# Bias rows of the neighbourhood attention loaded as 219 numbers in a row, and other rooms for the values and keys of the context's second quad

## The chip, the core and the metric

The kernel runs on one core of one Trainium2 chip. The core has TensorE (PE in the profile; PEld is its weight load), VectorE (DVE), ScalarE (ACT), GpSimd (POOL) and SyncE (SP), which here only issues DMAs. Each engine works through its own list of instructions in order and waits on semaphores; 16 DMA engines serve the transfers that SP, ACT and POOL issue. The metric is device time in microseconds (us) of one execution; lower is better.

## The reference, cut to what matters

A two-layer backbone works on 256 latent tokens (a grid of 4 rows x 64 columns) and 256 context tokens, 2048 features, fp32. The first layer joins two mixers; the change lies in both.

```python
# gated DeltaNet, 8 heads of 128, two directions; first over the context from a zero state,
# then over the latent tokens from the context's final state
def step(s, xc):                       # per chunk of 64 tokens
    v_new = u_c - einsum('bhik,bhkv->bhiv', w_c, s)
    s_next = s * exp(gl_c) + einsum('bhik,bhiv->bhkv', kd_c, v_new)   # keys and values of the chunk
# neighbourhood attention, 8 heads: every query sees all 4 grid rows, 16 columns, and all context keys
bias = rpb[:, dr[:, None, :, None], dc[None, :, None, :]]      # rpb: (8, 15, 31)
s_loc = einsum(q, k_window) * scale + bias
s_loc = where(in_win, s_loc, -inf)
p = softmax(concatenate([s_loc, q @ k_ctx]))
o = p_loc @ v_window + p_ctx @ v_ctx
```

Then come the output projection, a SwiGLU block, a short convolution layer and a second SwiGLU block, all large matmuls with weights read from HBM.

## The kernel before

**The matmul streams.** Weights come in tiles of 512 KB (`raw`, 4 buffers, loaded by SP at L235). ACT rounds each to `whi` (L175) and DVE forms the remainder `wlo` (L249), 3 buffers each; three products (high x high, high x low, low x high) give fp32 accuracy. The names KB, VB, QB and ZA are the streams of the attention's keys, values, queries and the DeltaNet's output gate; each takes eight tiles (ZA sixteen). The QB streams use 24 half-width matmuls (L347) for each tile. VB runs twice (L302, L303, L307, its last groups L319), and its results are staged in `nst` (3 buffers, copied at L170 or L172) and stored to `vb_d` (L1260). `araw`/`acc` (L435, L441, L443) is a side job: DVE sums the modulation weights while the streams run.

**The DeltaNet work between the streams.** A plan (`P_INV`) starts pieces of it after given steps of the streams. Heads go in two quads of four (q = 0, 1). `chunk_matrices(0)` prepares the latent chunks: DVE solves small triangular systems step by step (L1036 and L1038, tiles `sub_tmp` and `dgs`), which read `lsol`, loaded by SP in eight DMAs (L1027) from a DRAM tile `dl`; the solution goes back to DRAM in `dz` (L1045). `inverses` joins blocks (PE L1092, L1099, L1105; DVE L1107; ACT L1109) for one quad. `scan(q, 1, ...)` runs the context's recurrence of quad q: `kT`, `ktok` and `vtok` are loaded (L961, L956), then four steps of PE L1150 (value products), ACT L1154, PE L1158 (the state's update from `ktok`), DVE L1163, and from the third step on PE L1130 and DVE L1133 (tile `R`, from `vtok`). Both quads follow one another, and the latent quads later. `ktok` and `vtok` have one room each, so the second quad's loads wait until the first quad's last readers are done.

**The neighbourhood attention.** For each head `bias_rows` loads 6 x 64 numbers into each of 128 partitions, in two DMAs of 64 partitions (L1310), from the bias table: partition p starts p numbers further on, and the six pieces lie 31 numbers apart. `na_scores` adds the column mask in place on DVE (L1320), and PE adds the sum to the scores (L1324, L1325). The first head's bias load is issued once the VB stream has given up the memory in which the attention's tiles lie.

**What sets the order.** The tile framework schedules the instructions of all engines at build time, by simulated due times: a change of one room or one transfer changes the order on every engine. At run time each engine's order is fixed, and the SP list is one queue: a DMA that waits for a semaphore holds all those behind it.

Of the kernel before, what the change touches and what calls it, by code (L numbers as in the profile page):

```python
# [23 lines left out]
F32 = mybir.dt.float32  # L24
F32R = mybir.dt.float32r
AF = mybir.ActivationFunctionType
OP = mybir.AluOpType
# [84 lines left out]
def body(tc, x, c, ctx, c_ctx, ada_w, ada_b, norm_mix, norm_ffn, ffn_w_gate, ffn_w_up, ffn_w_down,  # L112
# [3 lines left out]
    PE, ACT, DVE, POOL, SP = nc.tensor, nc.scalar, nc.vector, nc.gpsimd, nc.sync  # L116
# [23 lines left out]
    def pool(name, bufs=1, stack=root, **kw):  # L140
        if kw.get("space") is not bass.MemoryType.DRAM:
            kw.setdefault("reuse_waits", "tile")
        p = stack.enter_context(tc.tile_pool(name=name, bufs=bufs, **kw))
        return p if "space" in kw else Rows(p)
# [15 lines left out]
    def smt():  # L160
        small.append(small.pop(0))
        return small[0].tile([128, 512], F32, name="sm", tag="sm")
# [11 lines left out]
    def acopy(dst, src):  # L174
        ACT.activation(dst, src, AF.Copy)  # L175
# [8 lines left out]
    def C(n):  # L184
        o, w = CO[n]
        return cs[:, o:o + w]
# [356 lines left out]
    def gdt():  # L543
        return gdp.tile([128, 512], F32, name="gd", tag="gd")
# [18 lines left out]
    p = smt()  # L563
# [114 lines left out]
    kd = dram.tile([128, 4, 8, 128], F32, name="kd")  # L678
    vd_ = dram.tile([128, 4, 8, 128], F32, name="vd_")
# [4 lines left out]
    def hslice(d_, t0, n, q):  # L684
        return d_[:, t0:t0 + n, q * 4:q * 4 + 4, :].rearrange("p t h e -> p t (h e)")
# [125 lines left out]
    for b in range(8):  # L811
# [4 lines left out]
        p = smt()  # L816
# [119 lines left out]
    def g4(name, tag, bufs=1):  # L936
        return gw.tile([128, 1024], F32, name=name, tag=tag, bufs=bufs)

    def g2(name, bufs=G2):
        return gw.tile([128, 4, 128], F32, name=name, tag="m2", bufs=bufs)  # L940
# [10 lines left out]
        ACT.activation(em, pD.rearrange("p (i e) -> p i e", i=4), AF.Exp)  # L951
        return em

    def load_tok(tag, d_, t0, q):
        t = g4(tag, tag).rearrange("p (t h e) -> p t h e", t=2, h=4)
        SP.dma_start(t.rearrange("p t h e -> p t (h e)"), hslice(d_, t0, 2, q))  # L956
        return t

    def load_feat(tag, src, pool_=None, bufs=1):
        t = (pool_ or gw).tile([128, 1024], F32, name=tag, tag=tag, bufs=bufs).rearrange("p (h t) -> p h t", h=4)  # L960
        SP.dma_start(t, src)  # L961
        return t
# [149 lines left out]
    def scan(q, seq, xdT, AT=None, qT=None, kT=None, o_t=None):  # L1112

        hs = [q * 4 + i for i in range(4)]
        if kT is None:
            kT = load_feat("kT", kTd[:, seq, q * 4:q * 4 + 4, :])
        ktok = load_tok("ktok", kd, 2 * seq, q)
        vtok = load_tok("vtok", vd_, 2 * seq, q)
        visited = set()
        for step in range(2):  # L1120
            for d in range(2):
                ti = step if d == 0 else 1 - step
                tt = 2 * seq + ti
                tok = slice(ti * 128, ti * 128 + 128)
                zero = seq and step == 0
                sv = state[:, d, q * 4:q * 4 + 4, :]
                if not zero:
                    pP = gdt()
                    for i in range(4):
                        PE.matmul(pP[:, i * 128:(i + 1) * 128], kT[:, i, tok], sv[:, i, :], start=True, stop=True)  # L1130
                    R = g2("R")
                    for i in range(4):
                        DVE.scalar_tensor_tensor(R[:, i, :], pP[:, i * 128:(i + 1) * 128],  # L1133
                                                 negegc[:, d, tt, hs[i]:hs[i] + 1], vtok[:, ti, i, :],
                                                 op0=OP.mult, op1=OP.add)
                if not seq:
                    pQ = gdt()
                    for i in range(4):
                        PE.matmul(pQ[:, i * 128:(i + 1) * 128], qT[:, i, tok], sv[:, i, :], start=True, stop=True)
                    for i in range(4):  # L1140
                        o = o_t[:, ti, i, :]
                        e = eg[:, 0, d, tt, hs[i]:hs[i] + 1]
                        if tt in visited:
                            DVE.scalar_tensor_tensor(o, pQ[:, i * 128:(i + 1) * 128], e, o, op0=OP.mult, op1=OP.add)
                        else:
                            ACT.activation(o, pQ[:, i * 128:(i + 1) * 128], AF.Copy, scale=e)
                pY = gdt()
                for i in range(4):
                    rhs = vtok[:, ti, i, :] if zero else R[:, i, :]
                    PE.matmul(pY[:, i * 128:(i + 1) * 128], xdT[:, d * 8 + ti * 4 + i, :], rhs, start=True, stop=True)  # L1150
                if seq or step == 0:
                    vd = g2("vd")
                    for i in range(4):
                        ACT.activation(vd[:, i, :], pY[:, i * 128:(i + 1) * 128], AF.Copy,  # L1154
                                       scale=brest[:, d, tt, hs[i]:hs[i] + 1])
                    pS = gdt()
                    for i in range(4):
                        PE.matmul(pS[:, i * 128:(i + 1) * 128], ktok[:, ti, i, :], vd[:, i, :], start=True, stop=True)  # L1158
                    if zero:
                        acopy(sv, pS.rearrange("p (i e) -> p i e", i=4))  # L1160
                    else:
                        for i in range(4):
                            DVE.scalar_tensor_tensor(sv[:, i, :], sv[:, i, :], eg[:, 2, d, tt, hs[i]:hs[i] + 1],  # L1163
                                                     pS[:, i * 128:(i + 1) * 128], op0=OP.mult, op1=OP.add)
                if not seq:
                    vn = g2("vn")
                    for i in range(4):
                        ACT.activation(vn[:, i, :], pY[:, i * 128:(i + 1) * 128], AF.Copy,
                                       scale=beta[:, d, tt, hs[i]:hs[i] + 1])
                    pA = gdt()  # L1170
                    for i in range(4):
                        PE.matmul(pA[:, i * 128:(i + 1) * 128], AT[:, d * 8 + ti * 4 + i, :], vn[:, i, :], start=True, stop=True)
                    ov = o_t[:, ti]
                    DVE.tensor_tensor(ov, ov, pA.rearrange("p (i e) -> p i e", i=4), op=OP.add)
                visited.add(tt)
# [12 lines left out]
    lgo = pool("gdn_out", stack=lgs, side="right")  # L1188
# [110 lines left out]
    nap = pool("na", stack=nastk)  # L1299
    yhi[1] = gw.tile([128, 4, 256], F32R, name="yhi1", tag="ktok", bufs=1)  # L1300
    ylo[1] = pool("y_lat", stack=lgs, side="right").tile([128, 4, 256], F32R, name="ylo1")
    bandf = C("band")
    bqs, scaled = {}, []

    def bias_rows(h):
        bq = bqs[h] = nap.tile([128, 6, 64], F32, name="bq", tag="bq", bufs=3)
        for half in range(2):
            src = bass.AP(tensor=ev_rpb.tensor, offset=ev_rpb.offset + h * 465 + (5 - half) * 31 + 15 - 63,
                          ap=[[1, 64], [31, 6], [1, 64]])
            SP.dma_start(bq[half * 64:half * 64 + 64], src)  # L1310

    def na_scores(h):
        kb = nap.tile([128, 512], F32, name="kb", tag="kb", bufs=2)
        qb = pairs[h // 2][:, h % 2, :]
        SP.dma_start(kb, kb_d[:, h, :])
        bq = bqs.pop(h)
        if h < 7:
            bias_rows(h + 1)
        with tc.issue_after(scaled[-1]) if scaled else Stack():
            DVE.tensor_tensor(bq, bq, bandf[:, None, :].to_broadcast([128, 6, 64]), op=OP.add)  # L1320
        out_ = []
        for t in range(2):
            p = smt()
            PE.matmul(p, qb[:, t * 128:(t + 1) * 128], kb, start=True, stop=False)  # L1324
            PE.matmul(p[:, 0:256], C("flip"), bq[:, 2 - 2 * t:6 - 2 * t, :].rearrange("p s c -> p (s c)"),  # L1325
                      start=False, stop=True)
            s = nap.tile([128, 512], F32, name="s", tag="s", bufs=4)
            m = nap.tile([128, 1], F32, name="m", tag="m", bufs=4)
            DVE.tensor_reduce(m, p, axis=AX.X, op=OP.max, negate=True)
            l = nap.tile([128, 1], F32, name="l", tag="l", bufs=4)  # L1330
            ACT.activation(s, p, AF.Exp, bias=m, accum_out=l)
            DVE.reciprocal(l, l)
            scaled.append(DVE.tensor_scalar(s, s, l, None, op0=OP.mult).ins)
            out_.append(s)
        return out_
# [29 lines left out]

    urgent[0] = True
    bias_rows(0)
    queries(0)
    held = na_scores(0)
    for h in range(8):  # L1370
        if h == 3:
# [266 lines left out]
    for half in range(2):  # L1638
# [8 lines left out]
        for f in range(8):  # L1647
            k = half * 8 + f
            p = smt()
# [64 lines left out]
```

## Time and profile before

| | us |
|---|---|
| median of 3 runs (lowest to highest) | 2704.55 (2703.65 to 2706.68) |
| profiled execution, its own time | 2704.46 |
| span of the profile, first to last instruction | 2702.7 |
| TensorE busy | 2643.9 (98% of the span) |
| VectorE busy | 1914.9 (71%) |
| ScalarE busy | 1275.3 (47%) |
| DMA, mean over the span | 253 GB/s |
| mean granted TensorE clock | 0.995 |

The profile is one execution. A group's line gives the source line (L...), the engine, the operation, its output and inputs, the count, the busy time and the mean of one; behind the bar or in brackets stands the engine's idle time before it and what ended it. The list of waits gives, for each pair, the total, the number of times and the longest. The granted clock is the share of TensorE's full clock that its throttle allowed.

### The profile page before, as it was taken

The numbers are of one execution on the slowest core, as the hardware profiler recorded it, in microseconds if no ns is written. First come the engines' busy times: TensorE is split into PE (matmuls) and PEld (weight loads), VectorE is DVE, ScalarE is ACT, GpSimd is POOL, SyncE is SP. The second block draws the span as 40 slices with busy tenths as digits, with TensorE's granted clock in tenths as the row PEclk, the third lists the DMA queues.
The fourth block names the chain that finished last, engine by engine and source line by source line (L and its number), as shares of the span: only waits on it lengthen the run. The fifth ranks groups of instructions, "written<-read, shape, count | busy, mean of one in ns | idle before, by whom it ended". The sixth has DMA issues, their size and how long they took to land.

```text
span 2702.7 us, 37494 instructions
## 1 busy us (share of the span) xinstructions
PE 2643.9 (98%) x13775; PEld 2181.4 (81%) x13775; DVE 1914.9 (71%) x2645; ACT 1275.3 (47%) x1848; POOL 47.1 (2%) x73
## 2 busy tenths in 40 slices
PE   6999999989999999999999999999999999999998
PEld 4688888888888888888888878888788888888886
DVE  4378798856698866776788878898575655545665
ACT  3258633334455444444455563444454444445554
POOL 0000101100000000000000000000000000000000
PEclk9999999999999999999999999999999999999999
DMA  9955688986596978888887859997577777666553
GB/s 368 356 157 177 186 274 263 302 266 186 184 336 230 340 280 289 296 288 287 281 293 260 301 173 337 334 339 253 170 251 224 235 228 238 211 200 213 195 194 110
DMA packets 285148, 682.71 MB, mean 253 GB/s; under 512 B 56957, under 2 KB 98581, under 8 KB 283555
## 3 DMA queue, kind: packets, MB, share of 16 engines
q1 hardware_dynamic: 278636, 667.14, 73.8%
q10 hardware_dynamic: 4423, 9.50, 1.0%
q0 software_dynamic: 1904, 3.67, 0.4%
q8 instruction: 108, 1.77, 0.3%
q14 instruction: 77, 0.63, 0.1%
HBM read 658.16 MB, written 22.05 MB: 252 GB/s over the span
## 4 chain that ended last, share of the span: by engine, by line
PE 92%; DMA 3%; DVE 2%; ACT 1%; issue 1%; SPq 0%; DVEq 0%; ACTq 0%
PE mm L302 21%; PE mm L307 21%; PE mm L303 21%; PE mm L347 11%; PE mm L319 8%; PE sm L194 2%; DMA araw<-in_ada_w_dram 1%; PE sm L605 1%; DVE wlo L249 1%; PE gd L347 1%; PE gd L949 1%; PE sm L1324 1%; PE gd L1150 1%; PE sm L1348 0%; DMA xn<-in_ctx_dram 0%
## 5 line engine op out<-in xcount | busy, mean ns | idle before, releaser
L249 DVE TENSOR_TENSOR wlo<-raw,whi 128x1024 fp32r<-128x1024 f32 x800 | 972.5, 1223 | 456.3 <-ACT whi L175 444.9
L175 ACT ACTIVATE whi<-raw 128x1024 fp32r<-128x1024 f32 x800 | 843.9, 1062 | 856.5 <-PE mm L307 632.9
L302 PE MATMUL mm<-whi,fhi 128*128 128x512 f32 x1232 | 481.9, 393 | 2.6 <-DVE fhi L1471 2.6
L303 PE MATMUL mm<-wlo,fhi 128*128 128x512 f32 x1232 | 479.7, 390 | 0.5 <-DVE wlo L249 0.5
L307 PE MATMUL mm<-whi,flo 128*128 128x512 f32 x1232 | 390.0, 390 | 0.0
L407 DVE SCALAR_TENSOR_TENSOR acc<-araw,cT,acc 128x1024 f32<-128x1024 f32 x224 | 286.8, 1281 | 35.7 <-DMA araw<-in_ada_w_dram 30.7
L302 PEld LDWEIGHTS mm<-whi,fhi 128*128 128x128 f32 x1232 | 231.3, 188 | 50.8 <-DVE fhi L1471 3.9
L307 PEld LDWEIGHTS mm<-whi,flo 128*128 128x128 f32 x1232 | 231.1, 188 | 48.4
L303 PEld LDWEIGHTS mm<-wlo,fhi 128*128 128x128 f32 x1232 | 231.3, 188 | 47.8 <-DVE wlo L249 1.2
L302 PE MATMUL mm<-whi,ahi 128*128 128x512 f32 x664 | 259.0, 390 | 0.0
L303 PE MATMUL mm<-wlo,ahi 128*128 128x512 f32 x664 | 258.3, 389 | 0.0
L347 PE MATMUL mm<-hB,whi 128*128 128x512 f32 (+1 forms) x840 | 234.5, 366 | 1.0 <-DVE hB L629 1.0
L307 PE MATMUL mm<-whi,alo 128*128 128x512 f32 x664 | 206.5, 389 | 0.0
L347 PEld LDWEIGHTS mm<-hB,whi 128*128 128x128 f32 x840 | 147.8, 189 | 24.5 <-DVE hB L629 2.3
L178 ACT ACTIVATE ahi<-prodT 128x256 fp32r<-128x256 f32 x176 | 73.0, 418 | 182.9 <-PE mm L303 179.3
L347 PE MATMUL mm<-hB,wlo 128*128 128x512 f32 (+1 forms) x420 | 149.8, 365 | 0.0
L307 PEld LDWEIGHTS mm<-whi,alo 128*128 128x128 f32 x664 | 124.7, 188 | 25.9
L302 PEld LDWEIGHTS mm<-whi,ahi 128*128 128x128 f32 x664 | 124.7, 188 | 25.8
L303 PEld LDWEIGHTS mm<-wlo,ahi 128*128 128x128 f32 x664 | 124.7, 188 | 25.6
L441 DVE SCALAR_TENSOR_TENSOR acc<-araw,cT,acc 128x512 f32<-128x512 f32 x180 | 133.9, 747 | 4.2 <-DMA araw<-in_ada_w_dram 3.4
L302 PE MATMUL mm<-whi,dhi 128*128 128x512 f32 x336 | 131.1, 393 | 1.2 <-DVE dhi L1471 1.2
L303 PE MATMUL mm<-wlo,dhi 128*128 128x512 f32 x336 | 130.7, 390 | 0.0
(410 smaller groups left out, 3516.4 us busy)
## 6 DMA issues: line engine op xcount, KB each, us to landing
araw<-in_ada_w_dram SPq DMA_DIRECT2D x288, 512.0 KB, 5.2
raw<-in_ffn_w_down_dram SPq DMA_DIRECT2D x176, 512.0 KB, 4.6
raw<-in_ffn_w_gate_dram SPq DMA_DIRECT2D x160, 512.0 KB, 4.4
raw<-in_ffn_w_up_dram SPq DMA_DIRECT2D x160, 512.0 KB, 4.5
raw<-in_ev_w_in_dram SPq DMA_DIRECT2D x112, 512.0 KB, 4.9
araw<-in_ada_w_dram SPq DMA_DIRECT2D x192, 256.0 KB, 4.9
raw<-in_od_w_in_dram SPq DMA_DIRECT2D x96, 512.0 KB, 5.1
raw<-in_ev_w_out_dram SPq DMA_DIRECT2D x32, 512.0 KB, 6.4
```

Of the source, the lines that this page charges most:

```text
L175: ACT.activation(dst, src, AF.Copy)
L178: ACT.activation(hi, src, AF.Copy)
L194: return PE.transpose(dst, src, ident[:n, :n])
L249: last_lo[0] = DVE.tensor_tensor(lo, raw, hi, op=OP.subtract).ins
L302: PE.matmul(ps[ti][n], a, hi[:, n * 512:(n + 1) * 512], start=first, stop=False)
L303: ins = PE.matmul(ps[ti][n], a, lo[:, n * 512:(n + 1) * 512], start=False, stop=False).ins
L307: last_mm[0] = PE.matmul(ps[ti][n], b, hi[:, n * 512:(n + 1) * 512], start=False, stop=False).ins
L319: ins = PE.matmul(ps[ti][n], a(t), w[:, c_], start=False, stop=a is ll and hi is group[-1][0]).ins
L347: last_mm[0] = PE.matmul(o, wt, h_(slice(0, len(ws)), mv, k), start=i == 0 and g == 0 and j == 0, stop=i == len(ks) - 1 and g == len(group ...
L407: DVE.scalar_tensor_tensor(acc, raw, cT[:, k:k + 1], acc, op0=OP.mult, op1=OP.add)
L441: DVE.scalar_tensor_tensor(accs[n], raws.pop(i), cT[:, k:k + 1], accs[n], op0=OP.mult, op1=OP.add)
L605: ins = PE.matmul(pr[32 * j:32 * j + 32, :], cT2[:, g + j, :], raw[:, j].rearrange("p s n -> p (s n)"), start=g == 0, stop=g == KT - 4).ins
```

## The change

`bias_rows` now loads 219 numbers in a row into each partition (tile `br`, 224 wide, 3 rooms): the six pieces of 64 that lie 31 apart overlap, and together they cover 5 x 31 + 64 = 219 numbers. The mask is added from overlapping windows of `br` into a tile `bq` of its own (2 rooms). In `scan`, the context's second quad gets other rooms: its keys go into the room `lsol` (free once the triangular solution is stored), its values into a room of `o_t` (two rooms; the preparation of the latent chunks used it for `n64`, and the latent outputs use it later).

```diff
-    def load_tok(tag, d_, t0, q):
-        t = g4(tag, tag).rearrange("p (t h e) -> p t h e", t=2, h=4)
+    def load_tok(tag, d_, t0, q, room=None):
+        t = (g4(tag, tag) if room is None else room).rearrange("p (t h e) -> p t h e", t=2, h=4)
...
-        ktok = load_tok("ktok", kd, 2 * seq, q)
-        vtok = load_tok("vtok", vd_, 2 * seq, q)
+        ktok = load_tok("lsol" if seq and q else "ktok", kd, 2 * seq, q)
+        vtok = load_tok("vtok", vd_, 2 * seq, q, lgo.tile([128, 1024], F32, name="vtok1", tag="o_t", bufs=2) if seq and q else None)
...
     def bias_rows(h):
-        bq = bqs[h] = nap.tile([128, 6, 64], F32, name="bq", tag="bq", bufs=3)
+        br = bands[h] = nap.tile([128, 224], F32, name="br", tag="br", bufs=3)
         for half in range(2):
             src = bass.AP(tensor=ev_rpb.tensor, offset=ev_rpb.offset + h * 465 + (5 - half) * 31 + 15 - 63,
-                          ap=[[1, 64], [31, 6], [1, 64]])
-            SP.dma_start(bq[half * 64:half * 64 + 64], src)
+                          ap=[[1, 64], [1, 219]])
+            SP.dma_start(br[half * 64:half * 64 + 64, 0:219], src)
+
+    def windows(br):
+
+        return bass.AP(tensor=br.tensor, offset=br.offset, ap=[list(br.ap[0]), [31, 6], [1, 64]])
...
-        bq = bqs.pop(h)
+        bq = nap.tile([128, 6, 64], F32, name="bq", tag="bq", bufs=2)
...
-            DVE.tensor_tensor(bq, bq, bandf[:, None, :].to_broadcast([128, 6, 64]), op=OP.add)
+            DVE.tensor_tensor(bq, windows(bands.pop(h)), bandf[:, None, :].to_broadcast([128, 6, 64]), op=OP.add)
```

The order changes on all engines in this part of the program. Three places matter.

On SP, ahead of the load of `lsol` for the triangular solution (the second quad's values are `vtok_4466` in the changed kernel):

```order
 L235 DMA raw<-in_ev_w_in_dram 128x2x512
 L961 DMA qT<-qTd 128x1024
+L956 DMA vtok_4466<-vd__152 128x2x512
 L1027 DMA lsol<-dl 16x32x32 x8
 L235 DMA raw<-in_ev_w_in_dram 128x2x512
```

The second quad's values now stand ahead of the eight loads of `lsol`, long before the scan.

On SP at the end of the VB stream, before:

```order
L1066 DMA xd<-dz 32x16x32 x2
L235 DMA raw<-in_ev_w_in_dram 128x2x512
L1066 DMA xd<-dz 32x16x32 x2
L1260 DMA vb_d<-nst 128x512
L435 DMA araw<-in_ada_w_dram 128x512
L1260 DMA vb_d<-nst 128x512 x2
L961 DMA kT<-kTd 128x1024
L1310 DMA bq<-in_ev_rpb_dram 64x6x64 x2
L956 DMA vtok<-vd__152 128x2x512
```

The same place in the changed kernel:

```order
L956 DMA lsol<-kd 128x2x512
L1066 DMA xd<-dz 32x16x32
L235 DMA raw<-in_ev_w_in_dram 128x2x512
L1066 DMA xd<-dz 32x16x32 x3
L435 DMA araw<-in_ada_w_dram 128x512
L1260 DMA vb_d<-nst 128x512 x3
L1310 DMA br<-in_ev_rpb_dram 64x219 x2
L1319 DMA kb<-kb_d 128x512
L961 DMA kT<-kTd 128x1024
```

The second quad's keys (`lsol<-kd`) have moved up ahead of `xd`, its values are gone from here, and the first head's bias rows stand ahead of `kT`, no longer behind it.

On DVE at the first bias addition, before:

```order
L1163 SCALAR_TENSOR_TENSOR state<-state,eg,gd 128x128 x4
L1133 SCALAR_TENSOR_TENSOR R<-gd,negegc,vtok 128x128 x4
L172 COPY nst<-mm 128x512
L249 TENSOR_TENSOR wlo<-raw,whi 128x1024
L441 SCALAR_TENSOR_TENSOR acc<-araw,cT,acc 128x512 x2
L1320 TENSOR_TENSOR bq<-bq,cs 128x384
L249 TENSOR_TENSOR wlo<-raw,whi 128x1024
```

And in the changed kernel:

```order
L1163 SCALAR_TENSOR_TENSOR state<-state,eg,gd 128x128 x4
L249 TENSOR_TENSOR wlo<-raw,whi 128x1024
L441 SCALAR_TENSOR_TENSOR acc<-araw,cT,acc 128x512
L1133 SCALAR_TENSOR_TENSOR R<-gd,negegc,vtok 128x128 x4
L172 COPY nst<-mm 128x512
L441 SCALAR_TENSOR_TENSOR acc<-araw,cT,acc 128x512
L1324 TENSOR_TENSOR bq<-br,cs 128x384
L249 TENSOR_TENSOR wlo<-raw,whi 128x1024
```

One `wlo` has moved ahead of `R`; in both orders 83 `wlo` stand ahead of the first bias addition, and the 84th directly behind it.

More of the change, by code (lines that the diff above doesn't have):

```diff
@@ L1302, in body @@
     bandf = C("band")
-    bqs, scaled = {}, []
+    bands, scaled = {}, []
     def bias_rows(h):
-        bq = bqs[h] = nap.tile([128, 6, 64], F32, name="bq", tag="bq", bufs=3)
+        br = bands[h] = nap.tile([128, 224], F32, name="br", tag="br", bufs=3)
         for half in range(2):
             src = bass.AP(tensor=ev_rpb.tensor, offset=ev_rpb.offset + h * 465 + (5 - half) * 31 + 15 - 63,
-                          ap=[[1, 64], [31, 6], [1, 64]])
-            SP.dma_start(bq[half * 64:half * 64 + 64], src)
+                          ap=[[1, 64], [1, 219]])
+            SP.dma_start(br[half * 64:half * 64 + 64, 0:219], src)
+    def windows(br):
+        return bass.AP(tensor=br.tensor, offset=br.offset, ap=[list(br.ap[0]), [31, 6], [1, 64]])
     def na_scores(h):
```

## The prediction

> **What bounds the kernel now.** I read the chain that ended last, then TensorE's waits, then the stretch of the longest one. The page first:
>
> ```profile
> span 2702.7 us, 37494 instructions
> PE 92%; DMA 3%; DVE 2%; ACT 1%; issue 1%; SPq 0%; DVEq 0%; ACTq 0%
> ```
>
> TensorE is the bound. The change takes no matmul away, so it can only return time in which TensorE stands still or runs at a reduced clock. TensorE's waits from 480 to 760 us, which hold everything that the change touches:
>
> ```profile
> PE gd L1150 <- DMA vtok<-vd__152: 7.2, 1, 7.2
> PE gd L1099 <- issue: 2.0, 1, 2.0
> PE gd L1105 <- issue: 1.8, 1, 1.8
> PE mm L347 <- DVE nst L172: 0.4, 1, 0.4
> ```
>
> The longest is the second quad's first product in `scan`, which waits for that quad's values. The chain in order of time and the granted clock there (columns: stretch, length, PE busy, clock, DMA share, GB/s):
>
> ```profile
> 552.14 2.87 PE mm L347 x24
> 555.01 0.67 PE gd L1150 x6
> 556.60 12.23 DMA vtok<-vd__152
> 568.87 2.07 PE gd L1150 x8
> 570.94 11.16 PE mm L347 x79
> 583.00 0.89 PE gd L1150 x8
> ...
> 562.00:564.00 2.00, 0.00 (x0) 1.00 0.65 121
> 564.00:566.00 2.00, 0.00 (x0) 0.61 1.03 384
> 572.00:574.00 2.00, 2.00 (x12) 0.50 0.50 64
> 574.00:576.00 2.00, 2.00 (x16) 0.83 0.85 272
> ```
>
> The values are issued at 556.60, when the one room is free, and come 12.23 us later. The idle array loses half its clock, and the half clock lasts some 6 us into the work that follows. Why they come so late shows in SP's list and in what the DMA engines moved from 557.5 to 563 us:
>
> ```profile
> 554.17 0.72 SPq L961 DMA_DIRECT2D kT<-kTd  x1
> 555.07 1.43 SPq L1310 DMA_DIRECT2D bq<-in_ev_rpb_dram  x2
> 556.60 0.56 SPq L956 DMA_DIRECT2D vtok<-vd__152  x1
> ...
> DMA packets 786, 0.50 MB, mean 90 GB/s; under 512 B 703, under 2 KB 703, under 8 KB 786
> ```
>
> Just ahead of the values stand the first head's bias rows: 2 x 64 x 6 = 768 pieces of 256 bytes. For 5.5 us nearly every packet is a small one, and the engines deliver 90 GB/s.
>
> **Part one, other rooms.** The second quad's values move from 556.60 to directly behind `qT` (470.76 below). A 512 KB transfer issued 85 us ahead of its reader is there in any case, so the wait goes: -7.21 us (568.87 less the end of the work before it; the list rounds to 7.2). The half clock behind it goes too: the first eight products cost 2.07 against 0.89 at full clock (-1.18), and the 79 matmuls 11.16 against 79 x 2.87 / 24 = 9.45 (-1.71). Together -10.10 us.
>
> A rule on the clock: the Trainium skill (TensorE: Matmul & The Clock Gate, Part 1: The HAM clock gate) says that the array falls to half clock after an idle window of about 3.4 us and needs about 3.4 us of work to rise. By that the half clock would cost at most 1.7 us instead of 2.89, an estimate from that page, and the whole 8.9. The rows decide: half clock from 568.87 to beyond 574.
>
> The keys go into the room of `lsol`, and SP waits at that load until `lsol` is stored in `dz`. Before, the next row on SP waited for the same store, so I cost it at nothing:
>
> ```profile
> SPq L1066 <- DMA dz<-lsol: 5.2, 1, 5.2
> ...
> 470.76 0.51 SPq L961 DMA_DIRECT2D qT<-qTd  x1
> 471.69 8.45 SPq L1027 DMA_DIRECT2D lsol<-dl  x8
> ...
> DMA packets 3512, 1.16 MB, mean 193 GB/s; under 512 B 3130, under 2 KB 3136, under 8 KB 3512
> ...
> 482.70 0.21 DVE L1036 TENSOR_TENSOR sub_tmp<-lsol,dgs 128x31 f32<-128x31 f32 x1 [1.96 <-DMA lsol<-dl]
> 516.19 1.29 DVE L1107 TENSOR_SCALAR xd<-gd 32x256 f32<-32x256 f32 x3
> 518.93 1.14 PE L1092 MATMUL gd<-xd,n 64*64 64x64 f32 x30
> ```
>
> What the move costs: the values stand ahead of the eight `lsol` loads, for which DVE already waits 1.96 us. 512 KB at the 193 GB/s of 478 to 484 us take 2.7 us; at the 384 of the best stretch above, 1.4. DVE is late by that much in the triangular solution, and all behind it on DVE with it. TensorE feels it first at L1107: that ends at 517.48 and its reader L1092 starts at 518.93, 1.45 us of cover. So 0 to 1.25 us; I take 0.6, the middle, as nothing tells the ends apart. Were the cover gone, all 2.7 would count. The `wlo` lie up to three tiles ahead of TensorE, so there I cost it at nothing.
>
> The other new waits, each behind work done long before: `ylo` of the attention now waits for the last read of the second quad's keys, and the latent output for the last read of its values; both belong to scans that stand earlier on TensorE than their writers. I cost them at nothing.
>
> **Part two, bias rows.** The sixteen loads stay sixteen issues on SP. The addition keeps 384 numbers; out of place instead of in place I take the same 0.55 us, within 0.1 either way, beside a DVE that has idle time (below). The pieces shrink from 768 to 128 for each head, the bytes from 197 KB to 112 KB. What it is worth hangs on DVE:
>
> ```profile
> L1310 SPq DMA_DIRECT2D bq<-in_ev_rpb_dram x16: 601/610/697, 555.1 to 662.4; - x16
> L1320 DVE TENSOR_TENSOR bq<-bq,cs x8: 551/552/559, 565.9 to 707.2; 128x384 f32<-128x384 f32 x8
> 565.91 0.56 DVE L1320 TENSOR_TENSOR bq<-bq,cs 128x384 f32<-128x384 f32 x1 [6.57 <-DMA bq<-in_ev_rpb_dram]
> 566.38 1.22 DVE L249 TENSOR_TENSOR wlo<-raw,whi 128x1024 fp32r<-128x1024 f32 x1
> 557.70 1.06 ACT L175 ACTIVATE whi<-raw 128x1024 fp32r<-128x1024 f32 x1 [0.44 <-PE mm L347]
> ```
>
> DVE stood 6.57 us for the bias, to 565.91, with the 84th `wlo` behind it, although its `whi` was made at 557.70. TensorE did not feel that, since it stood for the values. With these present it runs on and needs the 84th tile (the QB stream's fourth, since 80 go into the streams before) at 552.14 + 3 x 2.87 + 3 x 0.89 (one product and one update of the first quad, one product of the second) + 0.43 for `nst` = 563.9. The addition and the split take 567.60 - 565.91 = 1.69, so the bias must land by 562.2.
>
> When will it? Two things pull it forward. It no longer stands behind `kT`: 512 KB, 1.4 us at 384 GB/s. And its pieces: if time goes with their number, 5.5 x 128 / 768 = 0.9 us, so 565.91 - 1.4 - 4.6 = 559.9; if with the bytes, 5.5 x 112 / 197 = 3.1, so 562.1. Both make it, the second barely. I take 0 us, with 0 to 5.6 in the range (first rival).
>
> Are the engines able to feed a faster stretch? PE, PEld, DVE, ACT, POOL, clock, DMA share, GB/s:
>
> ```profile
> 552.00:582.00 30.00, 22.36 (x164) 21.95 (x163) 14.46 (x23) 8.63 (x14) 1.81 (x1) 0.83 0.85 247
> 582.00:612.00 30.00, 30.00 (x369) 27.58 (x371) 21.80 (x45) 14.88 (x33) 2.76 (x2) 1.00 0.91 274
> ```
>
> DVE is half idle in the first stretch. DMA moves 7.4 MB there; in 20 us that would be 370 GB/s, too much, but 1 MB of it (second quad's keys and values) is moved out ahead, and 320 GB/s with fewer small packets lies under the 384 seen. I cost the weights at nothing.
>
> **Sum.** -7.21 - 1.18 - 1.71 + 0.6 = -9.5 us against the profiled execution's 2704.46 (1.76 outside its span), which lies 0.09 under the median of the runs: 2695.0.
>
> **Rivals.**
>
> *The bias takes the place of the values (0.14).* If the bias lands as late as before, at 565.91, TensorE waits from 563.9 for a `wlo` until 567.6: 3.7 us, and 1.9 for the clock (between the 0.74 that the row below shows and 2.89). That leaves 3.9 of 9.5: 2700.6. For it speaks that 256-byte pieces were slow for another reason than their number: later, other small packets pass far faster, 1153 in 2.5 us (second row). The Trainium skill (DMA: Bandwidth & Descriptors, Why small descriptors are slow) gives a 256-byte packet only 27% overhead; by that rule fewer pieces would save little more than the bytes, which is the 562.1 above, on the edge. No row shows 876-byte pieces.
>
> ```profile
> 612.45 1.82 issue
> DMA packets 1199, 0.24 MB, mean 95 GB/s; under 512 B 1153, under 2 KB 1153, under 8 KB 1199
> 614.59 2.66 PE sm L1348 x8
> 634.65 1.92 PE sm L1348 x8
> ```
>
> *The two stops without a releaser go as well (0.10).* TensorE stops 1.82 and 1.96 us amid runs of tiny matmuls, and the products after the first cost 2.66 instead of 1.92. The first stands in a stretch full of small packets. Without both: 3.8 + 0.7 more, 2690.5. Against it: the new order puts the same tiny matmuls as close together as the old.
>
> *`lsol` comes much later (0.05), and the kernel is slower.* If the values ahead of it take 12.23 us there as in the row above, DVE's solution, its store, SP's wait on that store and the bias behind it all move by 12.23; the bias then lands at 572.1, 9.9 us too late, and with 2.9 for the clock the gain of 10.1 turns into a loss of 2.7: 2707.2. It decides from a delay of 9.5 us on, and exceeds 0.2% from 14.9. Against it: no bias stands ahead of them at 470 us, and 384 GB/s would bring them in 1.4.
>
> **The numbers.** The forecast has 0.71, with 2692.5 to 2698 as its own range. The range runs from 2689.5, the second rival without the 0.6, to 2701, the first. 0.2% is 5.4 us, about what a measurement tells from no change: faster than 2699.1 are the forecast and the second rival, 0.81, less 0.01 for late weights; the first is within it, and half of the third: 0.15; slower 0.05.
>
> **What would show it.** Right: no wait of L1150 for `vtok`, a clock of 1.00 throughout 560 to 580, a bias load that lands in under 6 us, DVE's wait at the first addition under 3 us, under 200 packets below 512 bytes in the QB stream's first 10 us. Wrong: a wait of L347 for `wlo` after the first bias addition, a wait of L1092 for L1107 near 518, or of TensorE for `whi` later in QB, which would mean that weights became the bound.

## The result and the profile after

| | before | whole change |
|---|---|---|
| median on the chip of the prediction (20 runs each) | 2707.52 us | 2697.49 us |
| ratio (95% interval) | | 0.9967 (0.9959 to 0.9975) |
| the same, measured again twice (5 runs beside 23 each time) | 2708.73, 2707.12 us | 0.9964 (0.9952 to 0.9976), 0.9958 (0.9946 to 0.9970) |
| profiled execution: span, its own time | 2702.7, 2704.46 us | 2698.6, 2700.74 us |

The change saves 9 us, and between 7 and 11 (from the ratio; the two medians lie 10.0 apart). The three runs shown ahead of the prediction are among these twenty of the kernel before, whose median lies 3 us higher, so differences count, not absolute times.

The page of the profile after, its span and its chain by engine:

```profile
span 2698.6 us, 37488 instructions
PE 90%; DVE 3%; DMA 3%; ACT 1%; SPq 1%; issue 1%; DVEq 0%; ACTq 0%
```

TensorE is still the bound. Its waits from 480 to 760 us, the list that stood at the head of the prediction:

```profile
PE mm L347 <- DVE nst L172: 3.4, 1, 3.4
PE gd L1130 <- DMA kT<-kTd: 1.0, 1, 1.0
PE mm L347 <- issue: 0.6, 1, 0.6
PE gd L1150 <- DVE R L1133: 0.2, 1, 0.2
```

The 7.2 us for the second quad's values are gone, and of the two stops without a releaser (2.0 and 1.8) 0.6 is left. In their place stands a stop of L347 for `nst`, which was 0.4. The chain in order of time, then SP's list, then DVE's rows show where it comes from (the change moves the line numbers behind L1310 by 4):

```profile
543.57 13.35 DMA dz<-lsol
```

```profile
557.00 0.38 SPq L956 DMA_DIRECT2D lsol<-kd  x1
558.47 2.05 SPq L1066 DMA_DIRECT2D xd<-dz  x3
561.15 3.62 SPq L1260 DMA_DIRECT2D vb_d<-nst  x3
564.86 1.22 SPq L1310 DMA_DIRECT2D br<-in_ev_rpb_dram  x2
```

```profile
566.62 0.69 DVE L172 COPY nst<-mm 128x512 f32<-128x512 f32 x1 [6.10 <-DMA vb_d<-nst]
568.99 0.56 DVE L1324 TENSOR_TENSOR bq<-br,cs 128x384 f32<-128x384 f32 x1 [1.02 <-DMA br<-in_ev_rpb_dram]
```

`dz` takes 13.35 us to be stored. SP stands at the keys' load into `lsol` until then (8.9 us), and behind that row in the same list stand the loads of `xd` and the stores of `nst`. DVE cannot write the next `nst` until a room is free, and TensorE cannot start the next product. SP's rows in the kernel before:

```profile
549.66 0.86 SPq L1066 DMA_DIRECT2D xd<-dz  x2
552.19 0.43 SPq L1260 DMA_DIRECT2D vb_d<-nst  x1
553.19 0.89 SPq L1260 DMA_DIRECT2D vb_d<-nst  x2
```

By the time it reaches this part, the profile after runs 5.13 us later than the profile before (see below). Without that shift its first store of `nst` goes out at 556.0, which is 3.8 us later than before.

A second new wait lies far behind the change, at the end of the output projection:

```profile
844.13 1.26 PE L450 MATMUL sm<-cs,acc 128*128 128x1 f32 x8 [2.45 <-DVE acc L441]
846.57 0.63 PE L319 MATMUL mm<-wlo,yhi 128*128 128x512 f32 x1
```

The side job's last sum comes 2.45 us late, and the products behind run at half clock (0.63 for one in place of 0.39). In the new order this L450 stands 8 rows ahead of the next block's first product on TensorE, in the old one 36.

That the saving arises in the stretch that the change touches shows from the store of `n` (L1021) to the first product with `fhi`, one row of the kernel before and one of the profile after. Columns: stretch, its length, PE busy with its count, PEld, DVE, ACT, POOL, clock, DMA share, GB/s:

```profile
466.11:853.10 386.99, 372.32 (x3008) 318.60 (x3006) 286.46 (x535) 165.01 (x335) 12.75 (x14) 0.98 0.79 256
```

```profile
471.24:849.10 377.86, 369.74 (x3009) 317.58 (x3007) 288.25 (x536) 165.28 (x337) 13.37 (x14) 0.99 0.78 262
```

The same work takes 9.13 us less: TensorE stands 8.12 us instead of 14.67, and is busy 2.58 less. In the two other profiles of the whole change (`both` and `both2` below) it takes 375.3 and 375.4 us. Behind the stretch the two executions shown differ by 0.1 us (1849.6 and 1849.5). The start of the second row lies 5.13 later, and the two others of the whole change begin at 467.55 and 465.65: that shift arises ahead of the stretch and differs from run to run of one kernel, so it is not the change's.

### The profile page after: what moved, and what is told of

Same layout as the page of the kernel before. It is cut to its first block, busy times and chain, and to the rows that moved or that the text cites. A ratio compares the mean times of both kernels' runs of the same rounds, so it can differ in the third digit from the quotient of the medians.

```text
span 2698.6 us, 37488 instructions
## 1 busy us (share of the span) xinstructions
PE 2646.0 (98%) x13775; PEld 2183.0 (81%) x13775; DVE 1915.9 (71%) x2645; ACT 1274.9 (47%) x1848; POOL 47.8 (2%) x73
## 4 chain that ended last, share of the span: by engine, by line
PE 90%; DVE 3%; DMA 3%; ACT 1%; SPq 1%; issue 1%; DVEq 0%; ACTq 0%
PE mm L302 21%; PE mm L307 21%; PE mm L303 21%; PE mm L347 10%; PE mm L319 8%; PE sm L194 2%; PE sm L605 1%; PE gd L347 1%; DMA araw<-in_ada_w_dram 1%; DMA dz<-lsol 1%; DVE acc L441 1%; PE sm L1328 0%; PE gd L949 0%; DMA xn<-in_ctx_dram 0%; DVE wlo L249 0%
## 5 line engine op out<-in xcount | busy, mean ns | idle before, releaser
L347 PE MATMUL mm<-hB,whi 128*128 128x512 f32 (+1 forms) x840 | 234.6, 366 | 1.0 <-DVE hB L629 1.0
L347 PEld LDWEIGHTS mm<-hB,whi 128*128 128x128 f32 x840 | 147.7, 189 | 24.5 <-DVE hB L629 2.3
L347 PE MATMUL mm<-hB,wlo 128*128 128x512 f32 (+1 forms) x420 | 149.7, 365 | 0.0
```

The source lines that it names most:

```text
L347: last_mm[0] = PE.matmul(o, wt, h_(slice(0, len(ws)), mv, k), start=i == 0 and g == 0 and j == 0, stop=i == len(ks) - 1 and g == len(group ...
```

## The experiments

Twelve runs in three groups, two of them of the whole change itself (`both`, `both2`); each group has its own runs of the kernel before. Gains in us are (1 - ratio) x 2708, with the interval's ends behind.

**The parts apart.** One kernel with the rooms alone, one with the bias rows alone, one with the whole change but for the keys' room:

```diff
 rooms:        only load_tok, and the two loads in scan
 bias:         only bias_rows, windows, na_scores
 values_bias:  the whole change, with
-        ktok = load_tok("lsol" if seq and q else "ktok", kd, 2 * seq, q)
+        ktok = load_tok("ktok", kd, 2 * seq, q)
```

> The whole change again, as the yardstick for the other kernels on this chip. Both theories: 0.9967 of the kernel before, within 0.0008; TensorE without a wait of L1150 for vtok, but with a stop of about 3.4 us of L347 for nst L172 near 563 us (SP's list stands 9 us at the load of lsol for the store of dz, and the stores of nst stand behind it), and a clock near 0.92 after it.

> Rooms alone, bias rows as 6 x 64 pieces as before. SP's order is that of the whole change but for two bias loads. Theory A (the prediction's step 'part two is worth nothing'): as fast as the whole change within 1 us, 0.9967; the bias lands later, but TensorE stands for nst anyway and does not feel it. Rival B (the prediction's first rival): the first bias load takes 8 us instead of 4, DVE stands at the first addition until about 573 us instead of 569, a wlo behind it is late, L347 waits 2 to 4 us for wlo and the clock falls: 3 to 5 us slower than the whole change, 0.998 to 0.9985.

> Bias rows alone, rooms as before. SP's order is that of the kernel before. The second quad's values still wait for their room and are issued at about 556.6 behind the bias. Theory A: with 128 pieces instead of 768 ahead of them they land sooner by what the small pieces took less what 128 pieces take, 2.4 us (by bytes) to 4.6 us (by count): TensorE's wait for vtok is 2.6 to 4.8 us instead of 7.2 and the half clock mostly stays: 2.4 to 6 us gained, 0.9978 to 0.9991. Rival C (the bias has nothing to do with the values being late, the busy DMA engines alone hold them): within 0.5 us of before, 0.9998 to 1.

> The whole change without the keys' room: the second quad's keys stay in the room ktok, so their load stands some 20 places later on SP, behind the bias rows and the loads of xdT. Theory A (the prediction priced the keys' move at nothing because the next row on SP waits for the same store): the stop for nst stays at 3.4 us within 0.5, no other stop appears, time as the whole change within 1 us. Rival D (the keys' room is worth its place): the load comes at about 577 us and lands 4 to 6 us later, L1158 of the second quad waits for ktok 4 to 6 us, 4 to 7 us slower than the whole change. Rival E (the load of lsol is itself what holds the stores of nst): the stop for nst is under 2 us and the kernel 2 to 4 us faster than the whole change.

| | ratio | gain, us |
|---|---|---|
| whole change | 0.9964 (0.9952 to 0.9976) | 9.7 (6 to 13) |
| rooms | 0.9987 (0.9978 to 0.9996) | 3.5 (1 to 6) |
| bias | 0.9981 (0.9970 to 0.9991) | 5.1 (2 to 8) |
| values_bias | 0.9963 (0.9951 to 0.9975) | 10.0 (7 to 13) |

The whole change's stop for `nst` was 0.4 us in this profile, where 3.4 had been expected, and 1.5 us of waiting for `R` came behind it; in the third profile it was 3.4 again. The stop is real and varies from run to run.

*Rooms alone* has the same order on SP in this stretch, but for two bias loads. TensorE's waits from 560 to 640, then the landing of its sixteen bias loads (least, median, most) and that of the whole change:

```profile
PE gd L1150 <- ACT state L175: 4.3, 1, 4.3
PE mm L347 <- DVE nst L172: 3.8, 1, 3.8
PE mm L347 <- DVE wlo L249: 0.9, 1, 0.9
```

```profile
DMA to landing us min/median/max: 5.5/9.2/10.7
```

```profile
DMA to landing us min/median/max: 3.1/5.0/6.2
```

Theory A is out. The time is near rival B's (6 us behind the whole change, where it said 3 to 5), though by another way than the one written down. The wait for `wlo` is only 0.9. The rest comes through late loads: with 768 small pieces a head among them, `kT` takes 7.85 us (4.67 in `both`), and the loads behind it come one after the other, up to a weight tile whose `whi` stands on ACT ahead of the copy that L1150 waits for. The chain in order of time:

```profile
564.33 7.85 DMA kT<-kTd
572.18 8.85 DMA vtok<-vd__152
...
583.71 4.43 DMA raw<-in_ev_w_in_dram
```

*Bias alone* shows the other half: the order of before, and the values still waited for. Its waits, then on the chain the load's length and the products behind:

```profile
PE gd L1150 <- DMA vtok<-vd__152: 3.2, 1, 3.2
PE gd L1105 <- issue: 2.1, 1, 2.1
```

```profile
562.44 7.09 DMA vtok<-vd__152
569.58 2.08 PE gd L1150 x8
```

The values come 7.09 us after their issue instead of 12.23, and the wait and the time are theory A's. The half clock behind the values stays (2.08 for eight products), and so does a stop without a releaser; in the profiles with the rooms this wait is gone, and the stops without a releaser are 1.2 us at most. This kernel also stands 4.7 us at the end of the output projection, where L194 waits for `rtmp`; the rooms alone and the whole change stand 2.5 us there, at L450. The gains of the parts hold what each order costs at that place.

*values_bias* waits where rival D said, and is no slower, as theory A said; its stop for `nst` is 1.0, under the 2 of rival E and not theory A's 3.4, but without rival E's gain. TensorE's waits and SP's:

```profile
PE gd L1158 <- DMA ktok<-kd: 4.6, 1, 4.6
PE mm L347 <- DVE nst L172: 1.0, 1, 1.0
```

```profile
SPq L1066 <- DMA dz<-lsol: 5.0, 1, 5.0
```

The keys come 4.6 us late. SP stands 5.0 us for `dz` instead of 7.7 to 8.9, and the side job's wait at L450 does not arise in this order. What the keys' room saves it loses again elsewhere; the time does not tell the two apart.

**SP's stand, from four sides.** All are the whole change with other queues:

```diff
 stores_pool:  the four stores of nst in VB's second half
-            SP.dma_start(dst(i), st_)
+            (eng or SP).dma_start(dst(i), st_)          # eng = POOL
 keys_pool:    the second quad's keys
-        SP.dma_start(t.rearrange("p t h e -> p t (h e)"), hslice(d_, t0, 2, q))
+        (POOL if tag == "lsol" else SP).dma_start(t.rearrange("p t h e -> p t (h e)"), hslice(d_, t0, 2, q))
 loads_pool:   those keys, and the latent chunks' xd and xdT
-                SP.dma_start(m_, dz[v, b, q].rearrange("d t (r c) -> r (d t) c", r=32))
+                (eng or SP).dma_start(m_, ...)              # eng = POOL
```

> The whole change, with the four stores of nst in the VB stream's second half issued by POOL instead of SP; SP's order is otherwise that of the whole change. Theory A (the new stop of L347 for nst, 0.4 us in one profile of the whole change and 3.4 in the other, 3.8 with the rooms alone, comes from SP, which stands 8 to 9 us at the load of lsol for the store of dz, with the stores of nst behind it in the one list): the stop is gone, under 0.3 us, and the kernel is 0.5 to 4 us faster than the whole change, 0.9950 to 0.9962. Rival F (nst is late because the transfers themselves land late in that stretch): the stop stays, time as the whole change within 1 us.

> The whole change once more, beside the three kernels of this call. Both theories: 0.9965 of the kernel before, within 0.001; a stop for nst of 0.4 to 3.4 us near 562 us, the wait of L450 for acc (2.5 us near 841) and at most 2 us in stops without a releaser between 600 and 640.

> The whole change with the load of the second quad's keys (into lsol) issued by POOL; the loads of xd stay on SP. Theory A (the prediction's step: the wait at that load costs nothing on SP since the next row, xd<-dz, waits for the same store): SP stands at xd instead, for 5 us or more, the stop for nst stays between 0.4 and 3.4 us, time as the whole change within 1 us. Rival E (the keys' load is what holds the list): SP's wait is under 3 us, no stop for nst, 1 to 4 us faster than the whole change.

> The whole change with all loads that wait for the store of dz from the latent chunks (the keys into lsol, xd and xdT) issued by POOL, so that nothing on SP waits for it. Theory A (one cause stands behind the stop for nst, the late bias once the stores are out of the way, and the late weights after it: SP's stand of 8 to 9 us): no stop for nst, DVE's wait at the first addition of the bias under 2 us, no wait of L1150 for R near 580; 2 to 5 us faster than the whole change, 0.9945 to 0.9958. Rival H (POOL's issue of the 128-byte pieces of xd and xdT is slow, and L1092 of the latent quads waits for them): a wait of L1092 for xd or xdT of over 2 us between 590 and 640, time as the whole change or slower.

Ratios: stores_pool 0.9971 (0.9961 to 0.9981); the whole change beside the other two 0.9958 (0.9946 to 0.9970), keys_pool 0.9964 (0.9953 to 0.9976), loads_pool 0.9991 (0.9979 to 1.0002).

With the stores on POOL the stop for `nst` is gone, as theory A says, and the kernel is not faster. What is left on TensorE, DVE and SP:

```profile
PE gd L1150 <- DVE R L1133: 3.6, 1, 3.6
PE mm L347 <- DVE wlo L249: 0.7, 1, 0.7
DVE bq L1324 <- DMA br<-in_ev_rpb_dram: 6.6, 1, 6.6
SPq L956 <- DMA dz<-lsol: 8.2, 1, 8.2
```

DVE no longer stops at `nst`, so it reaches the bias 6.6 us ahead of the load, which stands behind SP's wait as the stores did. The late row is another one, with the same cause.

With the keys alone off SP, SP stands at the next row for the same store. Its 4.4 us lie between theory A's 5 or more and rival E's 3 or less, and the time is the whole change's:

```profile
SPq L1066 <- DMA dz<-lsol: 4.4, 1, 4.4
PE mm L347 <- DVE nst L172: 0.4, 1, 0.4
PE gd L1150 <- DVE R L1133: 1.8, 1, 1.8
```

With nothing left on SP that waits for `dz`, the stop for `nst` is gone, the first bias load goes out at 550.63, DVE waits 0.7 us for it and L1150 not at all for `R`. So the stand is the cause of all three. But rival H holds too: POOL issues the four loads of `xdT` one every 5.5 us or so, from 575.0 to 591.2 (SP issued four from 577.2 to 579.1 in the first profile after), and the chunk inverses wait.

```profile
PE gd L1099 <- DMA xdT<-dz: 7.5, 2, 6.4
DVE bq L1324 <- DMA br<-in_ev_rpb_dram: 0.7, 1, 0.7
```

This profile is of the fastest of its twelve runs (2697.4 against a median of 2706.1), so the wait can be longer in the others; the second kernel with these queues (below) shows 9.8.

How long TensorE stops for `nst` goes by when SP comes to the stores, not by how long SP stands. Counted from the store of `n`, the first of them goes out after 86 to 88 us where the stop is 0.4 (the kernel before, keys_pool, `both`), after 89 where it is 1.0 and 1.1 (values_bias, and a kernel named wide below), and after 90 to 91 where it is 3.4 to 3.8 (the two others of the whole change, rooms).

**Pieces or bytes.** The whole change, with 384 numbers in a row in place of 219: as many bytes as before, as few pieces as after; the second kernel has the queues of loads_pool besides.

```diff
-        br = bands[h] = nap.tile([128, 224], F32, name="br", tag="br", bufs=3)
+        back = 165 if h > 3 else 0
+        br = nap.tile([128, 384], F32, name="br", tag="br", bufs=2)
...
-                          ap=[[1, 64], [1, 219]])
+                          ap=[[1, 64], [1, 384]])
```

> The whole change, but each partition loads 384 numbers in a row instead of 219 (two rooms for br instead of three): 128 pieces for a head as in the whole change, 197 KB as in the kernel before. Theory A (the prediction's first price: a bias load's time goes with the number of its pieces): landing median 5 us as in the whole change, within 0.5. Rival B (the prediction's second price: it goes with the bytes): landing 8 to 9 us, as with 768 pieces of the same bytes (9.2 with the rooms alone), and 2 to 5 us slower than the whole change.

> As loads_pool, and bias rows of 384 numbers in a row (two rooms). Theory A: with SP free, the bias is early either way, so the width changes nothing: as loads_pool within 1 us. Rival: the shorter landing (3.1 us against 5) lets the queries' weights come sooner: 1 to 2 us faster than loads_pool.

0.9970 (0.9961 to 0.9980) for the first, the whole change's time. The landing of its sixteen loads:

```profile
DMA to landing us min/median/max: 2.7/3.1/7.1
```

One such load is half a head. The same bytes that land in 7.8 us (median, the kernel before) or 9.2 (rooms) as 384 pieces land in 3.1 as 64: the number of pieces counts, as theory A said. Not it alone, though, and the 5 us that theory A expected did not come: 64 pieces of 876 bytes took 4.0 to 6.2 in the kernels with such pieces, 64 of 1536 bytes 3.1 and, in the second kernel, 2.9. What makes the 876 slower was not tried. The second kernel measured 0.9993 (0.9982 to 1.0004), as loads_pool, and waits for `xdT` like it; on its own question it says little, since that wait covers the rest.

**The side job.** One number of the plan, and the same with stores_pool's edit:

```diff
-R_KB = 1.6
+R_KB = 1.8
```

> The whole change with the side job (the sums acc of the modulation weights) run 1.8 instead of 1.6 steps for each step of the KB and VB streams, so that its last close (L450) stands 116 rows ahead of the next block's first product instead of 8. Theory A (the wait of L450 for acc, 2.5 us near 841 us and the half clock behind it, is new since the change's order lets the side job fall behind): that wait is gone, 2.5 to 4 us faster than the whole change if nothing else moves. Rival G (araw and raw share the DMA engines, and more araw in the KB and VB streams makes weights or lsol late): the wait is gone but others take its place between 470 and 600 us, and the time is that of the whole change or up to 5 us more.

> Both remedies on the whole change: stores of nst issued by POOL, and the side job at 1.8 steps. If both theories A hold, their gains add: 3 to 8 us faster than the whole change, 0.9935 to 0.9955. If rival G holds for the side job, as slow as kb18.

The wait of L450 is gone in both. The first measured 0.9986 (0.9978 to 0.9995), 5 to 8 us slower than the whole change. Waits arise earlier, between 470 and 560 us, where the whole change had none:

```profile
PE gd L1092 <- DMA xd<-dz: 2.2, 1, 2.2
PE gd L194 <- DVE nt L994: 2.0, 1, 2.0
```

That is rival G; these two waits are 4.2 us, and the rest of the loss was not traced. Together with the stores on POOL it measured 0.9960 (0.9948 to 0.9972), within the interval of the whole change and not the 3 to 8 us beyond it that two gains would have added up to. No kernel tried beats the whole change by more than the measurement can tell.

## Why the prediction was right, and where it was not

The forecast was 9.5 us; 8.9, 9.7 and 11.4 were measured. By its steps:

- **The values' wait, -7.21.** Right. It is in no profile with the values' new room (rooms, values_bias, the whole change).
- **The half clock behind it, -2.89.** Gone at that place, but not always from the program. Clock of TensorE (the column behind POOL) after the new stop in the first profile after, where I had asked for 1.00 (the two other profiles have it there):

```profile
568.00:570.00 2.00, 2.00 (x13) 2.00 (x13) 1.01 (x2) 1.69 (x2) 0.00 (x0) 0.59 0.99 288
570.00:572.00 2.00, 2.00 (x13) 2.00 (x12) 2.00 (x3) 0.42 (x1) 0.00 (x0) 0.56 0.96 213
572.00:574.00 2.00, 2.00 (x19) 2.00 (x19) 1.88 (x6) 0.51 (x2) 0.00 (x0) 1.00 1.01 359
```

  Four microseconds at 0.59 and 0.56 lose 1.7, and the half clock at L450 another 1.6 (the work from 844.13 to 848.26 takes 2.5 at the lengths of the same products at full clock). Summed over the whole stretch, the time lost to the lower clock (busy time x (1 - clock), in steps of 1 us) is 4.6 us before, and 3.4, 1.7 and 0.0 in the three profiles of the whole change. The 4.6 are the 2.9 here and 1.7 behind a stop without a releaser, of which the prediction's second rival counted 0.7. So the term came out between -1.2 and -4.6, and differs from one execution to the next.
- **The values ahead of `lsol`, +0.6.** DVE's wait at the first L1036 rose from 1.96 to 3.1 us (2.7 to 3.4 in the other kernels with this room and the old side job): by 0.7 to 1.4, at or under the low end of the 1.4 to 2.7 that I priced. TensorE did not feel it at L1092: no profile of the whole change has a wait there, so it was 0 of the 0 to 1.25. Another way was not in the sum. Counted from the store of `n`, the store `dz<-lsol` goes out after 70.4 us before, and after 71.7, 70.9 and 72.3 in the three profiles of the whole change; SP's stand ends with that store, and the stop for `nst` is 3.4, 0.4 and 3.4 there. Whether the late `lsol` is what makes `dz` late was not tried.
- **The keys' room, 0.** In time it is 0, as values_bias and keys_pool show within 3 us. The reason that I gave is half right. The next row does wait for the same store, but not as long: 4.4 and 5.0 us against 7.7 to 9.1 in the six profiles with the keys on SP and the old side job. And I named nothing of what is queued behind, though the three stores of `nst` stood in the quoted rows, and TensorE's 0.4 us for `nst` in the first list. That is the step that failed: the sum left the stop for `nst` at its 0.4 us, and it was 3.4 in two of three profiles.
- **The bias rows, 0.** The price by the number of pieces is nearer to what wide shows than the one by bytes. The loads landed in 4.5 to 5.0 us (medians of the three profiles) and DVE waited 1.0 to 1.5 us for the first, as the signs asked. The place in time is not borne out. The load comes behind SP's stand: in the kernel before's time (less each profile's shift) the first addition began at 563.9, 561.3 and 564.0, later than the 559.9 forecast, and in two of three later than the 562.2 by which it was due. TensorE did not wait for the `wlo` behind it, since in those two it had itself lost 3.4 us to `nst`. That is luck, not the margin that I gave.
- **Small packets.** I asked for under 200 in the QB stream's first 10 us. There are 2229 in the first profile after, and 1825 at the same place before, as `xd` and its pieces of 128 bytes load there in both. That sign was badly chosen.
- **First rival, the bias takes the place of the values: 3.9 of 9.5 us left.** The rooms alone left 3.5 of 9.7. The price fits within the measurement (1 to 6) and the way was not right, as shown: late loads, more than the `wlo`.
- **Second rival, the stops without a releaser (0.10).** The stops went: 3.8 us before, 0.6, 1.2 and 0.5 in three profiles of the whole change. The time did not reach this rival's 2690.5, since new stops took as much. My reason against it, that the tiny matmuls stand as close as before, was no reason; they also moved among others. What ends these stops the traces do not show. The bias alone kept one of 2.1, and no profile with the rooms has one above 1.2, so it goes with the order that the rooms make; more was not tried.
- **Third rival, late `lsol`.** Did not come.

Two figures of the working are slightly off and change nothing: the second rival without the 0.6 is 2689.9, not 2689.5, and the first rival's 0.14, half of the third's 0.05 and the 0.01 for late weights give 0.175 for no change and leave 0.025 for slower, not 0.15 and 0.05.

So the size came out right partly by cancelling, and that part is luck. Of the standing time in the first profile after, not foreseen were 3.2 us of the stops without a releaser and 2.5 of waits near 780 (`o_t`, `ylo`, `yhi`) saved, and 3.0 at `nst`, 2.45 at L450 and 1.0 at `kT` lost. Of the 2.58 us of busy time the clock gives back 1.2; in the two other profiles busy time falls by 3.8 and 5.3, and the clock gives back 2.9 and 4.6. The rest, 0.7 to 1.4 us, is not resolved.

## What to carry to other kernels

When a DMA is moved to a place where it waits, read the rows behind it in the same list and who waits for each, even where the next row would have waited too: how long the list stands is one question, what stands in it another. Taking one late row out of such a list (stores_pool) only shows the next, and moving the waiters to a slower queue (loads_pool) moves the wait. Price a part of a change with and without the other part: the rooms alone, which take the whole wait for the values away, were worth 3.5 of 9.7 us, because late loads behind the small pieces took their place. The two parts alone add up to 8.6 us, which the measurement does not tell from the whole.

## What the hardware showed that was not expected

TensorE's clock can fall after stops far shorter than the 7.2 us of the kernel before, and the length of a stop alone does not decide it. The same six products (L1150) after stops of 1.53, 2.41 and 3.64 us, in `both`, in wide and in stores_pool:

```profile
580.61 0.91 PE L1150 MATMUL gd<-R,xdT 128*128 128x128 f32 x6 [1.53 <-DVE R L1133]
```

```profile
581.28 1.59 PE L1150 MATMUL gd<-R,xdT 128*128 128x128 f32 x6 [2.41 <-DVE R L1133]
```

```profile
581.68 1.62 PE L1150 MATMUL gd<-R,xdT 128*128 128x128 f32 x6 [3.64 <-DVE R L1133]
```

After 1.78 us in keys_pool they took 0.91 too. Elsewhere it is mixed. In the kernel before, the clock fell behind the stop of 1.82 us and not behind the one of 1.96. The third profile of the whole change has the same two stops as the first, 3.4 us for `nst` and 2.45 at L450, and its clock stays at 1.00 behind both, where the first fell to half behind both. Its stop for `nst` and the clock from the restart on:

```profile
561.72 0.50 PE L347 MATMUL mm<-hA,whi 128*128 128x256 f32 x2 [3.37 <-DVE nst L172]
```

```profile
562.00:564.00 2.00, 2.00 (x19) 1.00 0.90 307
```

So two executions of one kernel with the same stops differ by 3.4 us in the time lost to the clock. The Trainium skill (TensorE: Matmul & The Clock Gate, Part 1: The HAM clock gate) has the gate close after an idle window of about 3.4 us; these executions show it closing after stops of 1.82 to 2.45 us and staying open after one of 3.37, and the measurement decides. What decides between the two here the traces do not show.
